# Lo parts of the w_in and w_out blocks by an adding DMA instead of a DVE subtraction, in an encoder layer with two attention groups

## The chip, the cores and the metric

The kernel runs on one core of one Trainium2 chip. The metric is the device time of one execution in microseconds, the median of several runs. Its engines are called PE (TensorE, matrix products; PEld is its weight load), DVE (VectorE), ACT (ScalarE), POOL (GpSimd) and SP (SyncE, which here only issues DMAs). Each engine works through its own queue in order; semaphores tie the queues together.

## What is computed

One bidirectional encoder layer on x of 512 x 1024 in float32, cut to what matters:

```python
x = x + 0.5 * swiglu(rms_norm(x, ffn1_norm), w_gate1, w_up1, w_down1)
h = rms_norm(x, mix_norm)
proj = h @ w_in                       # 1024 x 2304: qa, ka, va, qb, kb, vb
oa = diff_attention(qa, ka, va)       # 8 heads, two softmaxes per head, relative bias
ob = gqa_attention(rope(rms(qb)), rope(rms(kb)), vb)   # 8 query heads, 2 key heads
x = x + concat(oa, ob) @ w_out        # 1024 x 1024
x = x + 0.5 * swiglu(rms_norm(x, ffn2_norm), w_gate2, w_up2, w_down2)
out = rms_norm(x, final_norm)
```

## The kernel before, in words

The large matrix products are made in a split form. A float32 operand w is written as hi + lo, where hi is w rounded to the engine's faster float32r format and lo = w - hi. One product then takes three matmuls: hi x hi, hi x lo and lo x hi (`mm3`, lines 213 to 216; the three have the lines 214, 215 and 216 in the profile). The attention itself uses the split only in part.

**Blocks of weights.** All weights pass through the class `Blocks` in blocks of 1 MB, in the order of the list `specs`: for each feed-forward part the gate and up blocks (11 each) and the down blocks d0 to d10, and between the two feed-forward parts nine blocks of w_in (va0, qk0, qk1, qk2, va1, qk3, kv, qb0, qb1) and four of w_out (o00, o01, o10, o11). `load` brings a block from HBM into a buffer `raw` by DMAs of the SP queue (line 92; the qk blocks by two DMAs, as their columns lie in two places). `convert` makes the pair hi and lo from it. raw, hi and lo have two buffers each. So block i+2 can be converted only when block i was read for the last time.

The kind "plain" is `plain` (line 114): in two halves, a cast on ACT that writes hi (line 100), and a subtraction on DVE that writes lo = raw - hi (line 101). Both lines are in `parts`, which other things use too. The kind "gate_up" (line 122) makes sums of quarter blocks first and isn't touched here.

`get(i)` (line 142) is called when the products of block i are about to be written. It converts block i and block i+1 and loads up to block i+2, at a high priority.

**Order of the work.** The framework orders the instructions of each engine at compile time, from priorities and a simulated time; the order of each queue is then fixed. `down` (line 417) multiplies the last two down blocks, d9 and d10, together for all four row groups (t = 2, 3, 0, 1), so that a row group is finished early. After each pair of row groups `mix_half` scales them by their norms, transposes them on PE (`half_T`, line 273; the matmuls of line 283, with the norm's power on POOL in line 262) and writes xm, the operand of the projections (lines 290 and 291).

**Projections and attention.** The projections of va0 (`proj_N`, line 588) and qk0 (`proj_qk`, line 557) run first, without anything beside them. Then a loop over 64 units (32 of group A, 32 of group B) writes scores, exponentials, joins, transposes and products with v. The other projections and the output projection are a stream of "filler" work which `fill` puts between the units in amounts from the list FILLS. A unit's parts are written with fixed lags: the join one unit after the scores (`A_join`, which for every third unit uses POOL in lines 732, 733 and 735; `B_join` with POOL in line 788), the transposes three units after (LAG_T), the products with v four units after. The scores of group A need the projected q and k rearranged in SBUF by DMAs (line 584).

In `proj_N` the weights' lo is the moving operand of the second matmul of every product; in `proj_qk` it is the stationary operand of the third.

Of the kernel before, what the change touches and what calls it, by code (L numbers as in the profile page):

```python
# [11 lines left out]
F32 = mybir.dt.float32  # L12
F32R = mybir.dt.float32r
AF = mybir.ActivationFunctionType
ALU = mybir.AluOpType
# [6 lines left out]
NK = D // P  # L22
# [49 lines left out]
class Blocks:  # L72
# [41 lines left out]
    def plain(self, t, shape, name):  # L114
# [4 lines left out]
            self.parts(hi[:, a:b, :], lo[:, a:b, :], t[:, a:b, :])  # L119
        return hi, lo  # L120

    def gate_up(self, t, shape, name):

        b11, b12, b21, b22 = t[:, 0:4, 0:P], t[:, 0:4, P:], t[:, 4:8, 0:P], t[:, 4:8, P:]
        hi, lo = self.pair(shape, name)
        T = {}
        for n, x, y in ((3, b22, b12), (1, b12, b11), (2, b22, b12), (4, b21, None)):
            if n != 1:
                T[n] = self.fpool.tile([P, 4, P], F32, tag="T", name=f"T{n}_{name}", bufs=3)
            eng = self.nc.gpsimd if n in (3, 2) else self.nc.vector  # L130
            eng.tensor_sub(b12 if n == 1 else T[n], x, T[2] if n == 4 else y)  # L131
        out = {1: (hi[:, 0:4, 0:P], lo[:, 0:4, 0:P]), 5: (hi[:, 0:4, P:], lo[:, 0:4, P:]),
               2: (hi[:, 4:8, 0:P], lo[:, 4:8, 0:P]), 3: (hi[:, 4:8, P:], lo[:, 4:8, P:])}
        self.parts(hi[:, 4:8, :], lo[:, 4:8, :], t[:, 4:8, :])
        self.parts(hi[:, 0:4, :], lo[:, 0:4, :], t[:, 0:4, :])
        for p, n in ((7, 3), (6, 2), (4, 4)):
            h, l = (self.fpool.tile([P, 4, P], F32R, tag=f"t{w}", name=f"t{w}{n}_{name}", bufs=4) for w in "hl")
            self.parts(h, l, T[n])
            out[p] = h, l
        return out  # L140
# [14 lines left out]
def build(ctx, tc, a, out):  # L155
# [24 lines left out]
    def add(key, name, kind, shape, parts):  # L180
        at[key] = len(specs)
        specs.append((name, kind, shape, parts))

    full = slice(None)
    for i in (0, 1):
        g, u, d = ffn[i]
        for j in range(NJ):
            for m, w in (("g", g), ("u", u)):
                cs = slice(256 * j, 256 * j + 256)
                if (i, j) == (0, 0):  # L190
                    parts = [((full, slice(0, 4)), w[:, 0:4, cs]), ((full, slice(4, 8)), w[:, 4:8, cs])]
                else:
                    parts = [(full, w[:, :, cs])]
                add((m, i, j), f"{m}{i}{j}", "gate_up" if j else "plain", [NK, 256], parts)
        for j in range(NJ):
            add(("d", i, j), f"d{i}{j}", "plain", [2, D], [(full, d[:, 2 * j:2 * j + 2, :])])
        if i == 0:
            cols = {"va0": 1024, "va1": 1280, "kv": 2048, "qb0": 1536, "qb1": 1792}
            for nm in ("va0", "qk0") + FILL_ORDER:
                if nm in cols:  # L200
                    parts = [(full, w_in[:, :, cols[nm]:cols[nm] + 256])]
                else:
                    c = P * int(nm[2])
                    parts = [((full, full, slice(0, P)), w_in[:, :, c:c + P]),
                             ((full, full, slice(P, 2 * P)), w_in[:, :, 512 + c:512 + c + P])]
                add(nm, nm, "plain", [NK, 256], parts)
            for part in (0, 1):
                for h in (0, 1):
                    add(("o", part, h), f"o{part}{h}", "plain", [4, 512],
                        [(full, w_out[:, 4 * part:4 * part + 4, 512 * h:512 * h + 512])])  # L210
    blocks = Blocks(tc, wpool, specs, AHEAD)

# [321 lines left out]

    L, second = first_half(gcol["ffn1"], "f1", keep_warm)
    H = gate_up(0, L, second, small_things)
    xg = []

# [449 lines left out]
    fpool = blocks.fpool = ffn_cm.__enter__()  # L988
    L, second = first_half(gcol["ffn2"], "f2")
    H = gate_up(1, L, second, None)  # L990
    G = fpool.tile([P, D], F32, tag="ut", name="G", bufs=1)
    nc.sync.dma_start(out=G, in_=a["final_norm"].partition_broadcast(P))
# [25 lines left out]
```

## Time and profile before

| what | value |
|---|---|
| runs | 1024.44, 1030.68, 1027.58 us; median 1027.58 |
| the profiled execution's own time | 1027.88 us |
| its span, first to last instruction | 1026.0 us |
| mean granted TensorE clock | 0.984 of full speed |
| busy PE, DVE, ACT, POOL | 993.7, 710.6, 486.0, 228.5 us |
| DMA traffic | 105.48 MB, mean 103 GB/s |

The span is cut by the profile into stretches. The first feed-forward part ends near 374 us, the projections begin there, the attention runs from about 413 to 657 us, and the second feed-forward part fills the rest. Times in rows are microseconds from the start of the span. In a row "out<-in" names the tile written and the tiles read, with buffer numbers left out (lo_qk stands for all four qk blocks); in brackets stands how long the engine was idle before the instruction, and what ended that idle time. The granted clock is a share of full speed: 1.00 is 2.4 GHz, 0.50 is 1.2 GHz.

### The profile page before, as it was taken

How to read it: one execution, taken by the hardware profiler on the slowest of the kernel's cores; microseconds unless marked ns; L12 is line 12 of the kernel's file. 1: busy time of each engine (PE TensorE's matmuls, PEld its weight loads, DVE VectorE, ACT ScalarE, POOL GpSimd, SP SyncE). 2: the span in 40 equal slices, each digit the busy share in tenths (PEclk: the TensorE clock that was granted, in tenths of full speed). 3: DMA queues.
4: the chain of work that ended last, by engine and by line, in shares of the span. 5: the costliest groups of instructions: out<-in, count | busy, mean ns of one | idle time of the engine just before them, and what ended most of it. 6: DMA issues, size and time to landing. Idle time of an engine off the chain costs nothing. (4 is left out here: it accounts for less than half of the span.)

```text
span 1026.0 us, 16988 instructions
## 1 busy us (share of the span) xinstructions
PE 993.7 (97%) x6700; PEld 915.0 (89%) x6700; DVE 710.6 (69%) x1152; ACT 486.0 (47%) x849; POOL 228.5 (22%) x222
## 2 busy tenths in 40 slices
PE   8999999999999999999998999799999999999997
PEld 7999999999888888899897778699999999988885
DVE  4898899988332253667897898559987888753124
ACT  6643454545231143667676567456444445532122
POOL 1143133230000000112465535112323232000000
PEclk9999999999999999999799999999999999999999
DMA  8143743332323333554432131113334242322312
GB/s 242 47 124 95 256 124 110 98 124 86 120 83 97 109 83 116 131 154 113 116 91 62 22 94 30 42 42 124 97 110 124 84 124 83 124 103 93 113 42 82
DMA packets 82400, 105.48 MB, mean 103 GB/s; under 512 B 7872, under 2 KB 66752, under 8 KB 82320
## 3 DMA queue, kind: packets, MB, share of 16 engines
q1 hardware_dynamic: 81744, 103.35, 32.6%
q8 instruction: 53, 0.87, 0.4%
q10 hardware_dynamic: 576, 1.05, 0.3%
q14 instruction: 27, 0.22, 0.1%
HBM read 93.86 MB, written 6.32 MB: 98 GB/s over the span
## 5 line engine op out<-in xcount | busy, mean ns | idle before, releaser
L131 POOL TENSOR_TENSOR T_g<-raw_g 128x512 f32<-128x512 f32 x40 | 68.7, 1719 | 190.7 <-DMA raw_g<-ffn_w_gate 95.1
L101 DVE TENSOR_TENSOR lo_d<-raw_d,hi_d 128x1024 fp32r<-128x1024 f32 x44 | 52.2, 1219 | 84.9 <-ACT hi_d L100 84.9
L100 ACT CAST hi_d<-raw_d 128x1024 fp32r<-128x1024 f32 x44 | 44.1, 1051 | 89.8 <-PE dn L216 87.3
L131 POOL TENSOR_TENSOR T_u<-raw_u 128x512 f32<-128x512 f32 x40 | 56.5, 1414 | 130.6 <-DVE tl_g L101 93.0
L100 ACT CAST th_u<-T_u 128x512 fp32r<-128x512 f32 x60 | 37.2, 620 | 88.9 <-PE cg L215 41.7
L100 ACT CAST th_g<-T_g 128x512 fp32r<-128x512 f32 x60 | 37.0, 617 | 51.0 <-PE cu L215 27.2
L101 DVE TENSOR_TENSOR lo_g<-raw_g,hi_g 128x1024 fp32r<-128x1024 f32 x44 | 54.1, 1232 | 5.7 <-ACT hi_g L100 5.6
L717 ACT ACTIVATE s_A<-s_A,m_A 128x512 f32<-128x512 f32 x64 | 46.4, 725 | 23.0 <-DVE m_A L715 19.5
L100 ACT CAST hi_g<-raw_g 128x1024 fp32r<-128x1024 f32 x44 | 44.3, 1048 | 26.1 <-PE dg L215 12.5
L101 DVE TENSOR_TENSOR lo_u<-raw_u,hi_u 128x1024 fp32r<-128x1024 f32 x44 | 53.3, 1215 | 1.4 <-ACT hi_u L100 1.4
L715 DVE CUSTOM_DVE_ANT_0 s_A<-sA,T 128x512 f32<-128x512 f32 x64 | 43.3, 684 | 12.2 <-PE sA L713 11.8
L100 ACT CAST hi_u<-raw_u 128x1024 fp32r<-128x1024 f32 x44 | 44.4, 1048 | 14.5 <-PE du L215 12.0
L101 DVE TENSOR_TENSOR tl_g<-T_g,th_g 128x512 fp32r<-128x512 f32 x60 | 51.1, 856 | 0.0
L101 DVE TENSOR_TENSOR tl_u<-T_u,th_u 128x512 fp32r<-128x512 f32 x60 | 50.9, 849 | 0.1
L788 POOL TENSOR_TENSOR p_B<-p_B,m_B 128x512 f32<-128x512 f32 x32 | 33.8, 1069 | 36.5 <-DVE m_B L787 34.3
L672 PEld LDWEIGHTS poA<-va,PT_A 128*128 128x128 f32 x256 | 36.0, 211 | 1.5 <-ACT PT_A L679 0.4
L672 PE MATMUL poA<-va,PT_A 128*128 128x64 f32 x256 | 35.9, 289 | 0.2 <-ACT PT_A L679 0.2
L262 POOL TENSOR_TENSOR r_mx<-r_mx,mhalf 128x1 f32<-128x1 f32 x4 | 2.2, 550 | 150.0 <-DVE r_mx L261 150.0
L262 POOL TENSOR_TENSOR r_fin<-r_fin,mhalf 128x1 f32<-128x1 f32 x4 | 2.2, 540 | 142.5 <-DVE r_fin L261 142.5
L713 PE MATMUL sA<-st_kqk,st_qqk 96*128 96x512 f32 x64 | 28.6, 461 | 1.1 <-DVE m_A L715 1.1
L782 ACT ACTIVATE p_B<-sB,m_B 128x512 f32<-128x512 f32 x32 | 22.1, 690 | 12.6 <-DVE m_B L779 10.7
L410 ACT ACTIVATE g<-g 128x1024 f32<-128x1024 f32 x20 | 21.2, 1061 | 13.8 <-DVE g L408 13.8
(700 smaller groups left out, 3872.1 us busy)
## 6 DMA issues: line engine op xcount, KB each, us to landing
raw_d<-ffn_w_down SPq DMA_DIRECT2D x22, 1024.0 KB, 4.9
raw_g<-ffn_w_gate SPq DMA_DIRECT2D x21, 1024.0 KB, 5.4
raw_u<-ffn_w_up SPq DMA_DIRECT2D x21, 1024.0 KB, 5.4
toep<-nbd SPq DMA_DIRECT2D x8, 512.0 KB, 8.3
raw_qk<-w_in SPq DMA_DIRECT2D x8, 512.0 KB, 5.5
raw_o<-w_out SPq DMA_DIRECT2D x4, 1024.0 KB, 5.6
T<-toep SPq DMA_DIRECT2D x8, 448.0 KB, 4.0
xn<-x SPq DMA_DIRECT2D x4, 512.0 KB, 6.0
```

The costliest lines, as they stand in the source:

```text
L100: self.nc.scalar.copy(out=hi, in_=src)
L101: self.nc.vector.tensor_sub(lo, src, hi.bitcast(F32))
L131: eng.tensor_sub(b12 if n == 1 else T[n], x, T[2] if n == 4 else y)
L262: nc.gpsimd.tensor_tensor(out=r, in0=r, in1=mhalf[:, 0:1], op=ALU.pow)
L410: nc.scalar.activation(g1, g1, AF.Silu)
L672: nc.tensor.matmul(ps, pt_sb[:, P * j:P * j + P], v(j), start=j == 0, stop=j == NT - 1)
L713: st["mm", n] = nc.tensor.matmul(ps, q4[h, s][:96, P * qt:P * qt + P], k4[h, s][:96, :], start=True, stop=True).ins
L715: nc.vector.tensor_tensor_reduce(out=sc, in0=ps, in1=T[:, 384 - P * qt:896 - P * qt], scale=1.0, scalar=BIG, op0=ALU.add, op1=ALU.min, acc ...
L717: nc.scalar.activation(sc, sc, AF.Exp, bias=m[:, s:s + 1], scale=-1.0, accum_out=l1[:, qt, h:h + 1] if s == 0 else l2)
L782: nc.scalar.activation(pm, ps, AF.Exp, bias=m[:, 0:1], scale=1.0, accum_out=m[:, 1:2])
L788: nc.gpsimd.tensor_mul(u["P"], u["P"], l.to_broadcast([P, S]))
```

## The change

The thirteen blocks of w_in and w_out get a new kind, "summed". hi is made as before. Then ACT writes -hi into lo, and when both halves of lo are written, a DMA issued by POOL reads the block from HBM once more and adds it onto lo in SBUF: lo = w - hi. The raw block is still loaded, since hi is made from it, but lo no longer reads it. A qk block takes two such DMAs, like its load. All other blocks and all other users of `parts` stay.

```diff
+    def summed(self, t, shape, name):
+
+        hi, lo = self.pair(shape, name)
+        step = (shape[0] + 1) // 2
+        for a in range(0, shape[0], step):
+            b = min(shape[0], a + step)
+            self.nc.scalar.copy(out=hi[:, a:b, :], in_=t[:, a:b, :])
+            self.nc.scalar.mul(lo[:, a:b, :], hi[:, a:b, :].bitcast(F32), -1.0)
+        for dst, src in self.specs[self.nsplit][3]:
+            self.nc.gpsimd.dma_start(out=lo[dst], in_=src, accum_op=ALU.add)
+        return hi, lo
...
-                add(nm, nm, "plain", [NK, 256], parts)
+                add(nm, nm, "summed", [NK, 256], parts)
             for part in (0, 1):
                 for h in (0, 1):
-                    add(("o", part, h), f"o{part}{h}", "plain", [4, 512],
+                    add(("o", part, h), f"o{part}{h}", "summed", [4, 512],
                         [(full, w_out[:, 4 * part:4 * part + 4, 512 * h:512 * h + 512])])
```

## Rows read from the trace of the kernel before

**Rows 1.** Part 1 of the page: busy us, share of the span, instructions.
```profile
PE 993.7 (97%) x6700; PEld 915.0 (89%) x6700; DVE 710.6 (69%) x1152; ACT 486.0 (47%) x849; POOL 228.5 (22%) x222
```

**Rows 2.** Busy us of the engines by stretch; then clock, DMA share, GB/s.
```profile
372.00:386.00 14.00, 12.65 (x96) 11.81 (x95) 9.62 (x18) 8.26 (x18) 0.55 (x1) 1.00 0.65 184
...
580.00:600.00 20.00, 20.00 (x113) 17.14 (x112) 19.84 (x39) 11.67 (x26) 11.10 (x13) 1.00 0.27 73
```

**Rows 3.** View of the va blocks' tiles: duration ns min/median/max, first and last start.
```profile
L100 ACT CAST hi_va<-raw_va x4: 1046/1049/1053, 372.1 to 414.4; 128x1024 fp32r<-128x1024 f32 x4
L101 DVE TENSOR_TENSOR lo_va<-raw_va,hi_va x4: 1212/1221/1226, 373.1 to 415.7; 128x1024 fp32r<-128x1024 f32 x4
L92 SPq DMA_DIRECT2D raw_va<-w_in x2: 367/442/518, 341.8 to 399.1; - x2
```

**Rows 4.** DMA issues: count, KB each, median us from issue to landing.
```profile
toep<-nbd SPq DMA_DIRECT2D x8, 512.0 KB, 8.3
...
raw_va<-w_in SPq DMA_DIRECT2D x2, 1024.0 KB, 5.9
...
st_kqk<-qk11h SPq DMA_DIRECT2D x8, 64.0 KB, 2.0
```

**Rows 5.** Timeline, 371 to 385 us: start, us, engine, line, operation.
```profile
371.41 0.39 PE L216 MATMUL dn<-hi_d,h09l 128*128 128x512 f32 x1
...
372.07 1.99 ACT L100 CAST hi_va<-raw_va 128x1024 fp32r<-128x1024 f32 x2
...
375.37 0.28 PE L215 MATMUL pva<-lo_va,xm 128*128 128x256 f32 x1
...
377.28 1.06 PE L283 MATMUL xt_mx<-diag_mx,xn 128*128 128x128 f32 x8
...
380.27 0.38 PE L216 MATMUL pva<-hi_va,xm 128*128 128x256 f32 x1 [1.22 <-DVE r_mx L261]
...
380.36 0.55 POOL L262 TENSOR_TENSOR r_mx<-r_mx,mhalf 128x1 f32<-128x1 f32 x1 [12.37 <-DVE r_mx L261]
...
383.36 1.95 PE L283 MATMUL xt_mx<-diag_mx,xn 128*128 128x128 f32 x16
```

**Rows 6.** Timeline, 394 to 426 us.
```profile
394.84 0.28 PE L215 MATMUL pva<-lo_va,xm 128*128 128x256 f32 x1
394.96 0.28 PE L216 MATMUL pva<-hi_va,xm 128*128 128x256 f32 x1
...
395.32 2.00 ACT L100 CAST hi_qk<-raw_qk 128x1024 fp32r<-128x1024 f32 x2 [7.57 <-issue]
...
403.04 0.39 PE L216 MATMUL pqk<-xm,lo_qk 128*128 128x512 f32 x1
...
413.24 0.39 PE L216 MATMUL pqk<-xm,lo_qk 128*128 128x512 f32 x1
...
425.72 0.28 PE L215 MATMUL pva<-lo_va,xm 128*128 128x256 f32 x1
```

**Rows 7.** Timeline: the second qb block's subtractions, POOL's additions there and at 423.
```profile
423.17 1.30 POOL L735 TENSOR_TENSOR pm_A<-pm_A,s_A 128x512 f32<-128x512 f32 x1 [2.38 <-DVE pm_A L734]
...
485.62 3.42 DVE L101 TENSOR_TENSOR lo_qb<-raw_qb,hi_qb 128x1024 fp32r<-128x1024 f32 x2
485.85 2.11 POOL L735 TENSOR_TENSOR pm_A<-pm_A,s_A 128x512 f32<-128x512 f32 x1 [1.05 <-PE poA L672]
...
488.02 0.72 PE L677 MATMUL pt_A<-ident,pm_A 128*128 128x128 f32 x4 [1.65 <-POOL pm_A L735]
```

**Rows 8.** Busy us by stretch around that place; the third number from the end is the clock.
```profile
490.00:492.00 2.00, 2.00 (x11) 2.00 (x11) 0.90 (x5) 1.27 (x4) 0.84 (x3) 0.50 0.98 347
...
502.00:504.00 2.00, 1.96 (x15) 1.48 (x15) 2.00 (x6) 1.79 (x7) 0.54 (x1) 0.97 0.43 98
```

**Rows 9.** Chain of waits that ended last, 350 to 700 us: start, us, what.
```profile
542.22 0.41 DVE lo_o L101
...
610.57 0.88 DVE lo_o L101
```

## The prediction, made blind

> **What bounds the kernel now.** I read the page's busy times first: TensorE (PE) is busy 993.7 of 1026.0 us, DVE 710.6, ACT 486.0, POOL 228.5 [rows 1]. So DVE time taken away is worth something only where PE waits for DVE, and a new wait of PE costs in full. The second view is the busy time by stretch. Around the start of the projections PE is busy 12.65 of 14 us and DVE 9.62; in the attention there is a stretch in which DVE has 19.84 of 20 us [rows 2]. The third view, the timeline, shows how a block of weights gets to PE. The hi and lo pairs have two buffers, so block i is converted when block i-2 has been read for the last time. For va0 that moment is the last product with block d9 at 371.41; ACT starts its two casts at 372.07 and PE multiplies by lo_va at 375.37 [rows 5]. Hardly any time lies between conversion and use there. Later there is more.
>
> **What is removed and added.** Thirteen blocks (nine of w_in, four of w_out), two halves each: 26 DVE subtractions of 1.22 us go, 31.7 us. 26 ACT multiplications by -1 come, of the casts' shape: 26 x 1.05 = 27.3 us [rows 3]. POOL gets 17 DMAs (qk blocks take two), and each waits until ACT has written both halves of -hi. The loads on SP stay as they are, since hi still comes from raw; 13.6 MB are read a second time. Three instructions in a row on ACT and DVE (cast, cast beside the first subtraction, last subtraction) become four on ACT and then one DMA: the latency of a block changes more than any engine's load.
>
> **The DMA's latency, D.** Nothing in the trace adds on the way, and POOL issues no DMA. From below: the plain load of the same block lands in 5.9 us. From above: the copies within HBM of 512 KB land in 8.3 us; with the 2.0 us that a 64 KB transfer takes as the fixed part, 1 MB would take 2.0 + 2 x 6.3 = 14.6 us, and with an issue of 0.5 us 15.1 [rows 3, 4]. The load is the nearer row (same source, same runs of 1 KB), but the add must also fetch -hi and so passes its moving part twice: 2.0 + 2 x 3.9 + 0.5 = 10.3 us, which I take. The next raw blocks and T tables load at the same time (the DMA engines are 65% busy there already [rows 2]), another reason not to take the low end.
>
> The Trainium skill (DMA: Bandwidth & Descriptors, Anatomy of one DMA) gives an estimate of 2.0 us plus bytes over 436 GB/s for a DMA issued by GpSimd, 4.4 us for 1 MiB; by it the sum would come out like the first rival below. The trace's plain load of 5.9 us is slower than that, though from another queue.
>
> **va0, step by step.** Four ACT instructions, each about 1.0 us, from 372.07: done at 376.1. Plus 10.3: lo_va lands at 386.4, where PE used it at 375.37, 11.0 us later. PE can do in the wait only what it did between: 16 transposes (1.9 us), the 8 before them (0.9), and the 1.2 us in which it was idle anyway [rows 5]: 4.0 us. PE's in-order queue stands 7.0 us. Behind POOL's waiting DMA stands the power for the row norms (380.36 [rows 5]); it and the squares on ACT can come up to 4 us later, still ahead of 386.4, so I cost them at nothing; with D at the low end that cover would be thin.
>
> **The clock.** At 488 PE had waited 1.65 us for POOL; then the granted clock fell to 0.50, that is 1.2 instead of 2.4 GHz, and was back only at about 502: some 13 us, 6.5 us lost [rows 7, 8]. The idle of 1.2 us at 380 [rows 5] was followed by no fall. For a stand of 7 us I bound the loss by 0 and 6.5 and take 5, as part of the low stretch falls into the wait itself. Together +12.0.
>
> **The blocks behind.** From a block's last product to the landing of its follower in the same buffer is 0.4 (394.96 to 395.32 [rows 6]) + 4.0 + 10.3 = 14.7 us.
> - qk1 waits for va0's buffer. va0's 96 products at 0.12 us [rows 6] take 11.5, with 5 for the clock: over at 402.9, so lo_qk1 lands at 417.6. PE would need it at 403.04 + 12.0 = 415.0 [rows 6]: +2.6, in all 14.6.
> - qk2 waits for qk0, over two products ahead of 403.04, 402.6 + 12.0: lands at 429.3; needed some 0.7 us after qk1's last product, 413.24 + 14.6 + 0.7 = 428.5 [rows 6]: +0.8, 15.4.
> - va1 waits for qk1, over at 413.5 + 14.6: lands at 442.8; needed at 425.72 + 15.4 = 441.1 [rows 6]: +1.7, 17.1.
> - qk3 and the rest: va1's products lie among attention units and its buffer cycle is longer than 14.7 us, so I cost them at nothing.
>
> **What comes back.** The chain of waits passes through lo_o twice, 0.41 + 0.88 us [rows 9]: -1.3. More hangs on one place. At 485.62 the two subtractions for a qb block take 3.42 us instead of 2.4, and POOL's addition beside them 2.11 instead of 1.30; PE waits 1.65 us for that addition, and the clock falls [rows 7, 8]. Taking the subtraction away removes 1.65 + 6.5 = 8.2 us if nothing takes its place. But POOL, the late engine, now has a DMA to issue for that block too. Bounds 0 and 8.2; I take half, 4, as one of two causes goes.
>
> The Trainium skill (SBUF, Who interferes with whom) says that a DVE instruction with two SBUF inputs holds up a GpSimd instruction that reads SBUF, and the 2.11 us agree. The same section says that descriptors for a GpSimd DMA can't be written while DVE runs in a two-port mode; by that the 4 us would shrink towards 0 and D grow. No row here shows it.
>
> **Other queues.** ACT's extra 2.1 us per block stand in front of exponentials; a unit is joined and transposed up to three units later, which hides that; without this cover it is 2.1 us for each of the seven late blocks. Behind POOL's DMAs stand the joins; their price, if late, is the wait of rows 7 again.
>
> Sum: 17.1 - 1.3 - 4 = +11.8 us on the profiled execution's 1027.88 us (span 1026.0 and 1.88 around it; the median of the runs is 1027.58, so it stands for them): **1039.7 us**. A measurement of this kernel tells about 0.5%, 5 us, from no change.
>
> **Rivals.**
> 1. *The DMA is as cheap as a load* (also what would be seen if it only wrote and did not add). D = 5.9: lo_va at 382.0, 6.6 us late, 2.1 of it filled, +4.5, with the clock's 0 to 5. The cycle of 10.3 us is shorter than a block, so no other block waits. With the 5.3 that comes back, or without: 1027 to 1037. For it: same bytes, same runs. Against: the second fetch. Chance 0.20.
> 2. *The DMA is dear.* D = 15.1: va0 +11.8 and 5; cycle 19.5; qk1 +7.3, qk2 +0.6, va1 +6.7, kv +1.2: +32.6, less 0 to 5.3: 1055 to 1060, and beyond if D is more. For it: the transfer in and out of HBM; writing descriptors for 1,024 runs on POOL, of which no row gives a price. Against: the load's row is nearer. Chance 0.23.
> 3. *Faster: the release of POOL and DVE at 485 decides.* It gives 8.2 + 1.3 = 9.5 us. It wins if lo_va lands by about 381.0 (D of 4.9), where PE stands 5.6 - 2.1 = 3.5 us without a fall of the clock: -6.0, 1021.9. For it: the wait is plainly tied to the subtraction. Against: D below the plain load's 5.9, and the order of POOL's work changes. Chance 0.10.
>
> **How the numbers follow.** The forecast's own case, D from 8 to 13, gives 1034 to 1050 and has 0.44; 0.03 is left for an order of instructions that hides the first wait and leaves the time as it is. Slower by over 0.5% (above 1032.7): the forecast's case, the dear DMA, and nearly half of the cheap one: 0.76. Within 0.5%: the other half and the 0.03: 0.14. Faster: 0.10. The range reaches from the cheap case's low end, 1026, to a little above the dear DMA's 1060, 1062; left out are the faster rival and the longest DMAs. Within the slower cases alone it would be 1033 to 1062.
>
> **What would show it.** In the profile of the changed kernel: ACT instructions of 1.05 us on lo tiles, no subtraction on them; a POOL DMA row whose landing gives D; PE idle before the first product with lo_va for about 7 us, ending on that DMA; a low granted clock behind it; short waits before qk1's and va1's lo; POOL's addition near 487 at 1.3 us. Wrong it would be if lo_va's landing is not what PE waits for, or if D lies outside 8 to 13.

## The result and the profile after

The changed kernel takes 1056.88 us (median of four runs, 1049.03 to 1059.15) against 1029.13 us for the kernel before in the same comparison: +27.75 us, a ratio of 1.0263 with a 95% interval of 1.0206 to 1.0319. The prediction was 1039.7 us in a range of 1026 to 1062. The sign and the range held; of the loss it saw less than half, 11.8 us of 27.75. The profiled execution took 1058.15 us, its span is 1056.4 us, 30.4 over the span before.

First the page: part 1, and of parts 2 and 3 the line of DMA totals and the line of the new queue on POOL. They answer to [rows 1].

```profile
PE 1006.3 (95%) x6700; PEld 925.6 (88%) x6700; DVE 681.8 (65%) x1126; ACT 510.1 (48%) x875; POOL 253.9 (24%) x239
...
DMA packets 98032, 119.12 MB, mean 113 GB/s; under 512 B 8144, under 2 KB 80336, under 8 KB 97952
...
q0 software_dynamic: 15632, 13.63, 8.8%
```

The exchange is as ordered: DVE 28.8 us less and 26 instructions fewer, ACT 24.1 us and 26 instructions more, POOL 17 instructions and 25.4 us more, 13.6 MB more moved. PE has the same 6700 matmuls, yet is busy 12.6 us longer. At equal work that points to the clock, which the stretches below show.

Now where the time went. The next two fences are the tile view's rows of the matmuls that read a lo part (durations in ns; then first and last start in us), of the kernel before and of the one after. The same products can be compared by their start.

```profile
L216 PE MATMUL pqk<-xm,lo_qk x64: 387/389/399, 387.4 to 462.0; 128*128 128x512 f32 x64
...
L215 PE MATMUL pkv<-lo_kv,xm x32: 278/283/364, 464.1 to 482.8; 128*128 128x256 f32 x32
...
L215 PE MATMUL pqb<-lo_qb,xm x64: 278/283/368, 505.9 to 540.6; 128*128 128x256 f32 x64
...
L215 PE MATMUL po<-lo_o,otB3h x8: 389/389/398, 646.2 to 657.3; 128*128 128x512 f32 x8
```

```profile
L228 PE MATMUL pqk<-xm,lo_qk x64: 387/389/482, 402.6 to 479.8; 128*128 128x512 f32 x64
...
L227 PE MATMUL pkv<-lo_kv,xm x32: 278/283/416, 483.9 to 504.3; 128*128 128x256 f32 x32
...
L227 PE MATMUL pqb<-lo_qb,xm x64: 278/283/415, 532.6 to 570.3; 128*128 128x256 f32 x64
...
L227 PE MATMUL po<-lo_o,otB3h x8: 389/389/398, 677.4 to 688.5; 128*128 128x512 f32 x8
```

The last product of the qk blocks starts 17.8 us later than before (479.8 - 462.0), the last of kv 21.5, the last of qb 29.7, the last of the output projection 31.2. POOL's first norm power behind the feed-forward part, which the change doesn't touch, is already 1.4 us later in this execution (362.80 against 361.37), so the lag that the change made is 16.4 us by the end of the qk blocks and 29.8 by the end of the output projection. Behind that nothing more is lost. The front and the attention have about half each in this execution.

The third view is the busy time of these two stretches as a whole, first of the kernel before, then after (columns as in [rows 2]; the third number from the end is the granted clock).

```profile
361.40:657.70 296.30, 284.63 (x1795) 251.03 (x1793) 214.88 (x491) 177.62 (x397) 94.92 (x124) 0.97 0.32 90
```

```profile
362.80:688.90 326.10, 297.82 (x1795) 261.63 (x1793) 185.26 (x465) 201.83 (x423) 121.01 (x141) 0.93 0.58 124
```

It is the same work, 1795 matmul records in both. PE stood idle 11.7 us before (296.3 - 284.6) and 28.3 after: 16.6 of the 29.8 us are waits, the other 13.2 are matmuls that ran longer at a lower clock, 0.93 on average instead of 0.97 (busy time times clock is 276 and 277 us).

Which waits these are, the timeline tells. At the front, where [rows 5] stood:

```profile
373.49 1.99 ACT L128 CAST hi_va<-raw_va 128x1024 fp32r<-128x1024 f32 x2
376.09 2.01 ACT L129 ACTIVATE lo_va<-hi_va 128x1024 fp32r<-128x1024 f32 x2
...
378.42 1.72 POOL L131 DMA_DIRECT2D lo_va<-w_in  x1 [9.01 <-ACT lo_va L129]
...
382.62 3.41 PE L295 MATMUL xt_mx<-diag_mx,xn 128*128 128x128 f32 x16 [4.73 <-DVE diag_mx L292]
...
389.42 0.55 PE L227 MATMUL pva<-lo_va,xm 128*128 128x256 f32 x1 [3.39 <-DMA lo_va<-w_in]
```

ACT needs from 373.49 to 378.1 for its four instructions, POOL issues the DMA at 378.42, and 11 us later PE goes on. In between it had only 16 transposes to do; the 4.73 us in front of them are part of the same stop, since before the change products with lo_va filled this time. Further on, waits of PE in the changed kernel (the bracket gives the idle time and what ended it), and the first products with qk1's and va1's lo part, at 413.79 and 441.60:

```profile
413.79 0.47 PE L228 MATMUL pqk<-xm,lo_qk 128*128 128x512 f32 x1
...
425.65 0.47 PE L228 MATMUL pqk<-xm,lo_qk 128*128 128x512 f32 x1 [0.45 <-DMA lo_qk<-w_in]
...
439.07 0.38 PE L226 MATMUL pva<-hi_va,xm 128*128 128x256 f32 x1 [1.62 <-DVE qk20l L587]
440.83 1.12 PE L689 MATMUL pt_A<-ident,pm_A 128*128 128x128 f32 x4 [1.38 <-POOL pm_A L747]
441.60 0.56 PE L227 MATMUL pva<-lo_va,xm 128*128 128x256 f32 x1
...
483.94 0.38 PE L227 MATMUL pkv<-lo_kv,xm 128*128 128x256 f32 x1 [1.85 <-DMA lo_kv<-w_in]
...
512.29 1.97 PE L684 MATMUL poA<-va,PT_A 128*128 128x64 f32 x8 [2.02 <-ACT PT_A L691]
...
572.71 0.50 PE L227 MATMUL po<-lo_o,ot 128*128 128x512 f32 x1 [1.81 <-DMA lo_o<-w_out]
...
591.27 1.19 PE L789 MATMUL sB<-k,ql 128*128 128x512 f32 x2 [3.90 <-DMA ql<-ql]
```

Four of the seven end on a DMA, three of them on an adding one. Those at 439 and 440 make one stop of 3.0 us. After every stop but the 0.45 us the clock fell, and once more after three short waits from 521 to 525 (1.08 us for POOL, 0.65 for DVE, 0.20 for ACT). Here are stretches behind va0, behind 440, 483 and 512, behind these three, and behind 572:

```profile
390.00:392.00 2.00, 2.00 (x11) 2.00 (x11) 0.00 (x0) 0.00 (x0) 0.00 (x0) 0.50 1.28 238
442.00:444.00 2.00, 2.00 (x10) 2.00 (x10) 0.16 (x1) 2.00 (x5) 0.00 (x0) 0.50 0.98 295
486.00:488.00 2.00, 2.00 (x10) 1.90 (x10) 0.04 (x1) 1.26 (x3) 0.00 (x0) 0.52 0.43 98
514.00:516.00 2.00, 2.00 (x9) 1.58 (x9) 1.93 (x8) 1.75 (x5) 0.72 (x1) 0.50 1.00 221
...
526.00:528.00 2.00, 2.00 (x12) 2.00 (x11) 2.00 (x8) 2.00 (x9) 1.12 (x3) 0.50 0.30 120
...
576.00:578.00 2.00, 2.00 (x9) 1.70 (x9) 0.20 (x1) 1.93 (x3) 0.00 (x0) 0.50 0.81 260
```

PE is busy all 2 us in each, at 1.2 GHz or little more. Taking PE's busy time times the missing share of the clock, stretch by stretch, the wait of 1.85 us at 483 cost 1.7 us more this way, and that of 1.81 us at 572 cost 3.3.

### The profile page after: what moved, and what is told of

Its sections match the earlier page's. It is cut to its first block, busy times and chain, and to the rows that moved or that the text cites. A ratio compares the mean times of both kernels' runs of the same rounds, so it can differ in the third digit from the quotient of the medians.

```text
span 1056.4 us, 17004 instructions
## 1 busy us (share of the span) xinstructions
PE 1006.3 (95%) x6700; PEld 925.6 (88%) x6700; DVE 681.8 (65%) x1126; ACT 510.1 (48%) x875; POOL 253.9 (24%) x239
## 3 DMA queue, kind: packets, MB, share of 16 engines
q10 hardware_dynamic: 576, 1.05, 0.3%
## 4 chain that ended last, share of the span: by engine, by line
PE 39%; DVE 4%; DMA 2%; issue 2%; ACT 2%; POOL 1%; POOLq 0%; DVEq 0%; ACTq 0%
PE dn L227 3%; PE dn L226 3%; PE dn L228 3%; PE po L227 1%; PE po L226 1%; PE poA L684 1%; PE cg L226 1%; PE du L228 1%; PE du L227 1%; PE du L226 1%; PE cu L228 1%; PE cu L227 1%; PE cu L226 1%; PE bu L228 1%; PE bu L227 1%
## 5 line engine op out<-in xcount | busy, mean ns | idle before, releaser
L100 ACT CAST hi_u<-raw_u 128x1024 fp32r<-128x1024 f32 x44 | 44.4, 1048 | 14.5 <-PE du L227 12.0
L791 DVE TENSOR_REDUCE m_B<-sB 128x1 f32<-128x512 f32 x32 | 22.0, 686 | 16.9 <-PE sB L789 16.6
L794 ACT ACTIVATE p_B<-sB,m_B 128x512 f32<-128x512 f32 x32 | 22.1, 691 | 15.3 <-DVE m_B L791 14.5
## 6 DMA issues: line engine op xcount, KB each, us to landing
lo_qk<-w_in POOLq DMA_DIRECT2D x8, 512.0 KB, 10.1
```

What stands on the lines that cost most here:

```text
L100: self.nc.scalar.copy(out=hi, in_=src)
L794: nc.scalar.activation(pm, ps, AF.Exp, bias=m[:, 0:1], scale=1.0, accum_out=m[:, 1:2])
```

## The experiments

All times are medians, each against the kernel before, measured beside it. That kernel's median was 1029.1 us beside the change, 1028.5 beside e4, e5, e2 and e3, 1027.5 beside e10, e9, e1 and e7, and 1028.7 beside e6 and e11. Every edited kernel is ordered anew by the framework, so differences of a few microseconds can also come from another order in a queue; no run separates that.

| run | what is different | us | ratio, 95% interval |
|---|---|---|---|
| the change | 13 blocks by the adding DMA | 1056.9 | 1.0263 (1.0206 to 1.0319) |
| e4_no_dma | no DMA, lo stays -hi | 1029.6 | 1.0019 (1.0006 to 1.0031) |
| e5_copy_dma | POOL's DMA copies instead of adding | 1039.6 | 1.0112 (1.0080 to 1.0144) |
| e10_copy_act | a copy inside SBUF from ACT's queue | 1037.2 | 1.0100 (1.0079 to 1.0120) |
| e9_half_dma | each adding DMA cut in two | 1047.8 | 1.0199 (1.0175 to 1.0224) |
| e6_act_and_dve | -hi by ACT, DVE adds, no DMA | 1032.6 | 1.0029 (1.0014 to 1.0044) |
| e1_va0_plain | va0 by subtraction | 1043.9 | 1.0176 (1.0141 to 1.0211) |
| e7_front_plain | first five blocks by subtraction | 1038.8 | 1.0102 (1.0074 to 1.0130) |
| e2_win_only | w_out by subtraction | 1046.7 | 1.0192 (1.0156 to 1.0228) |
| e3_wout_only | w_in by subtraction | 1034.1 | 1.0057 (1.0038 to 1.0075) |
| e11_mid_only | only qk3, kv, qb0, qb1 by the DMA | 1031.7 | 1.0039 (1.0024 to 1.0054) |

**Without the DMA.** Is it the DMA, or the load that moved from DVE to ACT?

```diff
-        for dst, src in self.specs[self.nsplit][3]:
-            self.nc.gpsimd.dma_start(out=lo[dst], in_=src, accum_op=ALU.add)
```

> Leaves out the addition: lo stays -hi, written by ACT; no DMA on POOL, no subtraction on DVE. What remains is the exchange of 31.7 us of DVE work for 27.3 us of ACT work. Theory (the landing of the adding DMA, 10.4 us after its issue, stops PE at va0 and holds up the blocks behind it, and these stops lower the clock): back at the kernel before or a little under it, 1021 to 1032 us. Rival (the load moved onto ACT holds up the exponentials and copies in the attention): the front, 16 us, is won back, but the part lost between 480 and 690 us, some 14 us, stays: 1038 to 1044 us.

1029.6 us: some 26 of the 27.75 us are gone. The rival falls; the load on ACT alone does not cost 14 us in the attention. The run also tells that DVE's relief, with ACT's load beside it, brings nothing in sum: without any subtraction on these blocks the time is 0.19% above the kernel before. The place of [rows 7] shows why. These rows are the timeline of PE in this run, with a step of the join on DVE ahead of the first, and a stretch behind:

```profile
486.53 0.49 DVE L744 TENSOR_SCALAR pm_A<-s_A,l_A 128x512 f32<-128x512 f32 x1 [0.64 <-POOL l_A L743]
487.91 0.50 PE L723 MATMUL sA<-st_kqk,st_qqk 96*128 96x512 f32 x1 [1.05 <-DVE m_A L725]
491.42 0.79 PE L723 MATMUL sA<-st_kqk,st_qqk 96*128 96x512 f32 x1 [1.15 <-DVE m_A L725]
```

```profile
494.00:496.00 2.00, 2.00 (x10) 1.82 (x10) 1.85 (x6) 2.00 (x6) 0.00 (x0) 0.50 1.03 343
```

The one wait of 1.65 us for POOL is replaced by two of 1.05 and 1.15 for DVE's maximum. In DVE's queue this maximum stands behind a step of the join, and that step had waited 0.64 us for POOL's factor l_A (0.57 the second time). The clock falls to 0.50 as it did before.

**ACT and DVE apart.** Splits this exchange.

```diff
             self.nc.scalar.mul(lo[:, a:b, :], hi[:, a:b, :].bitcast(F32), -1.0)
-        for dst, src in self.specs[self.nsplit][3]:
-            self.nc.gpsimd.dma_start(out=lo[dst], in_=src, accum_op=ALU.add)
+            self.nc.vector.tensor_add(lo[:, a:b, :], lo[:, a:b, :].bitcast(F32), t[:, a:b, :])
```

> ACT writes -hi as in the changed kernel, but DVE adds the raw block onto it (26 additions of the size of the old subtractions), and no DMA is issued: ACT has 27 us more than before, DVE as much as before. With the run without a DMA at +1 us, this splits the exchange. If DVE's relief was worth 5 us and ACT's load cost as much: 1032 to 1038 us. If neither counts: 1027 to 1032 us.

1032.6 us, at the lower edge of the first case; but its interval, 1.0014 to 1.0044, overlaps that of the run without a DMA, 1.0006 to 1.0031. The two can't be told apart. By the ratios DVE's relief is worth about 1 us (0.10%), by the medians 2.8, and ACT's load about 3 (0.29%), neither sure. Besides, this run puts DVE's addition behind ACT's multiplication, so a block's conversion is longer too; PE waits 0.7 us for it at va0.

**A copy in place of the addition.** What in the DMA is long?

```diff
-            self.nc.gpsimd.dma_start(out=lo[dst], in_=src, accum_op=ALU.add)
+            self.nc.gpsimd.dma_start(out=lo[dst], in_=src)
```

> The same DMAs issued by POOL at the same places, but plain copies that overwrite lo (leaves out the addition: lo is then the block itself). If the second fetch for the addition is what makes the landing long, the landing falls from 10.4 us to about 6 and the time to 1036 to 1046 us. If the path over POOL itself is long (1.6 us of issue, 1024 runs per block), the landing stays at 9 to 11 us and the time within 5 us of the changed kernel, 1052 to 1060.

1039.6 us. The tile view of lo_va, first of the changed kernel, then of this run (POOL's time for an issue in ns, min/median/max, and the landing):

```profile
L131 POOL DMA_DIRECT2D lo_va<-w_in x2: 1563/1642/1722, 378.4 to 431.2; - x2
...
DMA to landing us min/median/max: 9.9/10.4/10.9
```

```profile
L131 POOL DMA_DIRECT2D lo_va<-w_in x2: 876/986/1096, 379.1 to 427.8; - x2
...
DMA to landing us min/median/max: 6.9/7.3/7.6
```

The same bytes over the same queue land in 7.3 us as a copy and in 10.4 with the addition, and the issue takes 0.99 instead of 1.64 us. So the addition adds 3.1 us to va0's and va1's landing in the median (3.0 to 3.5 us by the DMA tables for qk, kv and w_out), and with the shorter issue this makes 17 of the 27.75 us. The case of the second fetch held by landing and time, with a landing a little above the 6 us expected; that it is the fetch of -hi that takes the 3 us, and not the addition itself, no run separates. The Trainium skill (Collectives: The Full Stack, The bandwidth ceiling: the fold count and why AG ≠ RS ≠ AR) says of a ReduceScatter that its add makes it slower because it needs two source reads and not because of the add itself, and finds half the rate of a plain copy; the trace agrees in direction, with 1.4 times the landing, fixed part included.

**A copy without POOL.** Is it the landing, or what POOL's queue holds up?

```diff
-        for dst, src in self.specs[self.nsplit][3]:
-            self.nc.gpsimd.dma_start(out=lo[dst], in_=src, accum_op=ALU.add)
+        for dst, _ in self.specs[self.nsplit][3]:
+            self.nc.scalar.dma_start(out=lo[dst].bitcast(F32), in_=hi[dst].bitcast(F32))
```

> Leaves out the addition: in place of the adding DMA a plain copy of hi onto lo inside SBUF, issued from ACT's queue behind its own instructions, so nothing is issued or waits on POOL. Theory (the landing alone): the time follows the landing, whichever queue issues it; with 5 to 6 us 1031 to 1037 us, with 7 us or more as much as the copy over POOL, 1036 to 1043. Rival (POOL's issue and the joins held up behind it): 1027 to 1031 us even if the landing takes 7 us.

The landing of lo_va (tile view) is much like that of the copy over POOL:

```profile
L131 ACTq DMA_DIRECT2D lo_va<-hi_va x2: 495/506/517, 377.9 to 429.4; - x2
...
DMA to landing us min/median/max: 6.9/6.9/6.9
```

And so is the time, 1037.2 against 1039.6 us, with overlapping intervals. With about the same landing and nothing at all on POOL the loss stays, so in the copy's 11 us POOL's issue and the joins behind it are not what costs. The rival falls for the copy; that the same holds for the adding DMA, with its longer issue, rests on the next run.

**Each DMA cut in two.** The landing from the other side: less latency with the same bytes.

```diff
             self.nc.scalar.mul(lo[:, a:b, :], hi[:, a:b, :].bitcast(F32), -1.0)
-        for dst, src in self.specs[self.nsplit][3]:
-            self.nc.gpsimd.dma_start(out=lo[dst], in_=src, accum_op=ALU.add)
+            for dst, src in self.specs[self.nsplit][3]:
+                self.nc.gpsimd.dma_start(out=lo[dst][:, a:b, :], in_=src[:, a:b, :], accum_op=ALU.add)
```

> Every adding DMA is cut in two, one for each half of the block, issued as soon as ACT has written -hi for that half. The bytes stay, the number of DMAs on POOL doubles. Theory (the time from conversion to the first usable half sets the stops): the first half lands about 4 us sooner and PE works on it while the second lands, so 8 to 15 us are won: 1042 to 1049 us. Rival (POOL's issue time, 1.6 us for each DMA, and what waits behind it): no gain or a loss, 1055 to 1064 us.

1047.8 us, 9 us less than the changed kernel by the medians and 6.6 by the ratios, whose intervals overlap slightly, though POOL issues 34 DMAs instead of 17 and is busy 270.6 us instead of 253.9. The first product with lo_va starts at 382.3 instead of 389.4; measured from POOL's first norm power (360.46 and 362.80) that is 4.8 us sooner. This is the theory's case.

**Which blocks.** Five runs put groups of blocks back to the subtraction by the kind given in `specs`; of these edits one stands here.

```diff
-                add(nm, nm, "summed", [NK, 256], parts)
+                add(nm, nm, "plain" if nm in ("va0", "qk0", "qk1", "qk2", "va1") else "summed", [NK, 256], parts)
```

> The first five blocks (va0, qk0, qk1, qk2, va1) go back to the subtraction; qk3, kv, qb0, qb1 and the four w_out blocks keep the adding DMA. Theory: the blocks whose buffers come free shortly before their use carry the front, 16 us of the 28; the other 12 us arise in the attention at kv, qb and o01 by themselves: 1036 to 1042 us. Rival (what is lost in the attention is only an echo of the late front): 1028 to 1034 us.

1038.8 us: without the first five blocks 11.4 us are left, and the first five have the other 16.4, the lag that the trace showed at the end of the qk blocks. Both intervals together leave some 10 to 23 us for these five, so the equal numbers are partly chance; but in this run's trace the last product of the qk blocks is not late at all (462.8 against 462.0, with the norm power 0.8 us later). The attention's part does not vanish with the late front, so it is no echo of it.

> Only va0 goes back to the subtraction; the other twelve blocks keep the adding DMA. Theory: PE's stop in front of va0 goes (lo_va is late by 12.6 us in the changed kernel, of which some is filled), but the adding DMAs of qk0 and qk1 land some 10 us after their -hi and PE meets them a little earlier, so part comes back there: 1042 to 1050 us. Rival (the first wait is only passed on to the next block): 1053 to 1058 us.

1043.9 us, in the theory's range. By the medians 13.0 us come back (1056.9 - 1043.9) and 9 by the ratios (2.63 - 1.76%), whose intervals overlap slightly. The time speaks for the theory; the trace of the front speaks for the rival. These are PE's waits there, from 370 to 400 and from 400 to 500 us, and the row of the products with lo_qk in this run:

```profile
PE pqk L228 <- DMA lo_qk<-w_in: 2.8, 1, 2.8
```

```profile
PE pva L227 <- DMA lo_va<-w_in: 3.7, 1, 3.7
PE pqk L228 <- DMA lo_qk<-w_in: 3.7, 1, 3.7
```

```profile
L228 PE MATMUL pqk<-xm,lo_qk x64: 389/389/797, 394.0 to 484.9; 128*128 128x512 f32 x64
```

Where the changed kernel waited 0.45 us for a lo_qk and not at all for va1's lo_va, this one waits 2.8, 3.7 and 3.7 us. Its last product of the qk blocks is 19.7 us behind the kernel before (484.9 - 462.0, less 3.2 us by which the norm power is later), no less than the 16.4 of the changed kernel; at the end of the output projection the lag is 17.4 instead of 29.8. So in this execution va0's wait is passed on to the blocks behind it, and what came back came back in the attention. It is the slowest of the run's four, 1050.6 us against 1043.5 to 1044.1, so how the others divide the gain stays open.

> The four w_out blocks go back to the subtraction, the nine w_in blocks keep the adding DMA. Theory: nearly all of the loss lies in the w_in blocks, since the lag against the kernel before is already 28 us at the last product of qb1; what w_out adds is one wait of 1.8 us for lo_o and a clock at half for 7 us behind it: 1046 to 1056 us. Rival (each block costs about alike, 28 us over 13 blocks): 1044 to 1050 us here and 1036 to 1040 in the run with w_out alone.

> The nine w_in blocks go back to the subtraction, the four w_out blocks keep the adding DMA. Theory: these blocks are converted some 17 us ahead of their first product, so a landing of 9.4 us is hidden but for the block whose buffer comes free late; DVE is relieved where it was at 19.8 of 20 us: 1022 to 1034 us. Rival (each block costs about alike): 1036 to 1040 us.

1046.7 and 1034.1 us. The w_in blocks have most of it, 18 of 27.75 us, but not nearly all: the first time lies in the theory's range and in the rival's. An equal share for each block falls with the second, 5.5 us where it gives 8.5; that run came out at the upper edge of what the theory gave, so these blocks are not free although they are converted early. One reason shows in their trace. These are the issues of qb's rearranged copies, 128 KB inside SBUF, in the DMA table of the kernel before, of the changed one, and PE's wait for one in the run with w_out alone:

```profile
ql<-ql SPq DMA_DIRECT2D x8, 128.0 KB, 2.2
```

```profile
ql<-ql SPq DMA_DIRECT2D x8, 128.0 KB, 4.0
```

```profile
PE sB L789 <- DMA ql<-ql: 2.4, 1, 2.4
```

The small copies run beside the adding DMAs and land in 4.0 instead of 2.2 us in the median (3.5 with w_out alone); PE waits 2.4 us for one of them there (1.1 before) and 3.9 in the changed kernel, each time while the adding DMA of a w_out block is in flight (issued at 548.99 with a landing of 11.4 us, and at 581.98 with 9.5).

> Only qk3, kv, qb0 and qb1 keep the adding DMA; the first five blocks and w_out have the subtraction. Theory (three parts that add up: front 16 us, these four blocks, w_out 5 to 6 us): the run with the first five blocks plain was 11 us over the kernel before, the one with w_out alone 5.5 us, so 4 to 8 us over it here, 1031 to 1036 us. Rival (no part of its own, the loss in the attention comes only with the w_out blocks): 1026 to 1030 us.

1031.7 us: +3.0, a little under the 4 to 8 us of the theory, though the time is in its range. The parts add up roughly: 16.4 (first five) + 3.0 + 5.5 = 24.9 of 27.75 us. That the last 2.9 us are a joint effect of the late blocks is likely, since the last two groups together (the run without the first five) cost 11.4 and one by one 8.5, but no run separates it from the scatter of some 1 to 2 us in each number.

## Why the prediction was right and where it was wrong

The direction and the range held, but the range, 1026 to 1062, is wide: it holds the front as it was forecast together with a loss in the attention that the sum had at nothing and even turned into a gain. That the time lies in it is no proof of the whole sum.

**Right: the step at va0 and D.** D was put at 10.3 us; it is 10.4 in the median of va0 and va1, 10.9 for va0 (over all blocks 6.5 to 15.0 for a DMA). ACT's four instructions took 4.6 instead of 4.0 us, as two other activations were ordered between them. lo_va's first product came 12.6 us late (389.42 - 1.43 - 375.37) where 11.0 were predicted, and PE stood 4.73 + 3.39 us, 6.9 more than the 1.22 before, where 7.0 were. The range of rival 2, 1055 to 1060, holds the measured time, but its cause is not the one at work: it needed a landing of 15.1 us.

**Right in part, and in its sum by luck: the blocks behind at the front.** Predicted were 17.1 us by va1; the lag at the end of the qk blocks is 16.4. The terms moved against each other. At qk1's first product with lo the lag is 9.3 us (413.79 - 1.43 - 403.04) where 14.6 were predicted, at qk2's 10.1 (425.65 - 1.43 - 414.17) instead of 15.4, at va1's 14.5 (441.60 - 1.43 - 425.72) instead of 17.1. The clock cost 2.7 us of PE's busy time from 382 to 394 instead of 5. qk1 and qk2, whose first DMAs landed in 6.5 and 7.8 us, were hardly waited for. At va1 the cycle did bind: its lo part landed at 441.1 (issued at 431.2, landing 9.9), and PE was through with qk2 at 437.3. But PE was held there by other things as well, the 1.62 us for a step of DVE that stores qk2's result and the 1.38 for a join that stands behind this step. The step writes into a buffer that the copies of qk00l read, and these landed in 7.8 instead of 5.0 us in the median; that they held it is likely, the profile doesn't name it. The fall of the clock behind 440 then added 2.0 us up to va1's last product. That the cycle is there shows best in the run with va0 put back, in which lo_qk and va1's lo_va are waited for (2.8, 3.7 and 3.7 us).

The cycle would also account for a loss that isn't in proportion to D: with 7.3 us it is 11 us, with 10.4 it is 28, and at the end of the qk blocks 6.6 against 16.4. The predicted cycle is 0.4 + 4.0 + D, which is 11.7 and 14.8, and a qk block's products take some 10.7 us (403.04 to 413.24 in [rows 6], and its first two); only what goes over that can become a wait. This is worked out; the waits themselves don't show it block by block.

**Wrong: "qk3 and the rest ... I cost them at nothing."** This step has the larger part of the error: measured are 11.4 us without the first five blocks, 3.0 of qk3, kv and qb alone and 5.5 of w_out alone. Its reason held for qk3 and the qb blocks, whose DMAs PE did not wait for. But kv's DMA took 13.1 us to land while the load of the next block and the rearranged q and k ran beside it, and PE stood 1.85 us; o01 stood 1.81; and the adding DMAs slowed the small copies on which scores wait. That transfers of others get slower beside these was seen for the raw loads only as a reason for a high D, not as a price of its own. What the short waits in the attention cost at the clock was left out with them.

**Wrong: "What comes back", -5.3 us.** The run without a DMA has no subtraction and is not faster, though ACT's load, some 2 to 3 us, may hide a part of what DVE's relief gives. The subtraction at 485 was the last thing to end the wait there, not the only one: with it gone POOL's addition takes 1.28 instead of 2.11 us, and PE stands for the next link, DVE's maximum, twice for over 1 us. For the -1.3 us of lo_o in the chain no run shows a gain either.

**Undersized: the clock.** One fall was priced, 5 us at va0. It cost 2.7 there, but over the whole stretch the longer matmuls make 13.2 us: each stop of 1.8 to 4 us in the attention was followed by several microseconds at half clock, and so were the three short waits before 525. A list of small waits has to be priced at their length and the clock's share together; here the waits were 16.6 us and the clock 13.2.

**ACT.** "2.1 us per block hidden by the units' lag" was nearly right: the two runs without a DMA lie 0.19 and 0.29% over the kernel before, 2 to 3 us. Once it is seen directly: at 512.29 PE stood 2.02 us for PT_A, whose copies stood behind the casts and multiplications of a qb block on ACT.

Left open: whether the conversion could be moved ahead far enough, say with a third pair of hi and lo buffers; no run tells. No version with the adding DMA beat the kernel before, and the exchange of ACT for DVE by itself brought nothing here.

## What to carry to other kernels

A step moved from an engine to a DMA is priced by its latency, not by the engine time it frees: ask how long the buffer cycle (last read, conversion, landing) is against the work that covers it, block by block, and count the slower landings of everything else on the same DMA engines. Work taken off an engine that ends a wait brings only the distance to the next thing that would have ended it. And where PE's clock falls behind its stops, as here, a short wait costs more than its length: 16.6 us of waits came with 13.2 us of longer matmuls.

## What the runs showed of the hardware

An accumulating DMA of 1 MB from HBM onto SBUF landed in 10.4 us where the copy over the same queue took 7.3, and held POOL for 1.64 instead of 0.99 us per issue of 1024 runs. No hold-up of POOL's issue by DVE showed: of two issues for w_out, that at 621.04 took 1.33 us with DVE busy all the time and that at 581.98 took 1.32 us with DVE idle; which forms of DVE's instructions could hold it up was not tested. In company the same DMA took up to 13.1 us (kv), one of 512 KB for a qk block up to 15.0, and copies of 128 KB inside SBUF went from 2.2 to 4.0 us. Short waits lowered the clock: the 1.81 us at 572 were followed by about 7 us at half clock, and in the run without a DMA two waits of 1.05 and 1.15 us by half clock too, while the 1.2 us at 380 in the kernel before had cost nothing.
